# A hand-ordered stage ahead of an RWKV-7 recurrence: scaled vectors moved between key tiles, mixes between gate products, triangular substitution spread over all receptance tiles on one engine

## The chip, the cores and the metric

The kernel runs on one core of a Trainium2 chip. The metric is device time in microseconds (us) of one execution, the median over several runs. Five engines work side by side, each through its own queue in order: PE (TensorE, the matmuls; PEld is its weight load), DVE (VectorE), ACT (ScalarE), POOL (GpSimd) and SP (SyncE, which issues the DMAs).

## What is computed

Two layers on a sequence of 512 tokens of width 1024: a gated short convolution with a squared-ReLU MLP, then an RWKV-7 time mixer with a second MLP. The change lies in the mixer, between its norm and its recurrence. From the normed `h` it computes, per token, six mixes of a token with the one before, and from these the vectors that the recurrence needs:

```python
h_prev = jnp.pad(h, ((0, 0), (1, 0), (0, 0)))[:, :-1]
xr, xw, xk, xv, xa, xg = h[None] + (h_prev - h)[None] * mu[:, None, None, :]
r, k, v = jnp.einsum('nbsd,nde->nbse', jnp.stack([xr, xk, xv]), w_rkv)
w = -jax.nn.softplus(-(w0 + jnp.tanh(xw @ w1) @ w2)) - 0.5
a = jax.nn.sigmoid(a0 + (xa @ a1) @ a2)
g = jax.nn.sigmoid(xg @ g1) @ g2
kk = heads(k * k_k); kk = kk / jnp.maximum(jnp.sqrt(jnp.sum(kk * kk, -1, keepdims=True)), 1e-12)
k = k * (1 + (a - 1) * k_a)
decay = jnp.exp(-jnp.exp(heads(w)))
y = _wkv7_scan(rh, decay, kh, vh, -kk, kk * ah)   # state <- state*w + (state a) b^T + v k^T, y = state r
```

## The kernel before

Activations lie feature-major: 1024 features are 8 blocks of 128 partitions, 512 tokens in the free dimension. A linear layer runs tile by tile: one tile is 128 output features, 8 blocks deep, and each weight and activation is kept as a high and a low part, so that `passes` (L171 to L173) issues three matmuls per block, 24 per tile. For each weight tile SP loads `raw` (two buffers), ACT rounds the high part (L131, cast) and DVE subtracts the low part (L132); `w_ahead` keeps this two tiles in front of PE.

The scan is done in 8 chunks of 64 tokens. For each chunk a 64x64 triangular system has to be inverted; its two 32x32 halves are inverted by substitution (`substitute`: for t from 30 down to 1, one multiply L849 and one add L853 on a block of t rows and 31-t columns), and joined by two small matmul levels (`inverse_level`). The stage ahead of the recurrence has these steps, which the string `PLAN` puts in an order by hand, one letter each; the order on PE is the order of the program, the other engines' queues are ordered by a scheduler:

- `K` key tile, of which five of eight are made with the norm before (`linear(NFIRST, ...)`); `key` copies the tile and squares it (ACT L601); `f` (`flush`) sums the squares per head on PE (L605); `n` (`inv_norms`) takes square roots (ACT L622) and reciprocals (DVE) of all that are there; POOL spreads a norm over its head's columns (L617)
- `T` output of the small decay and rate products, `W` their second product (PE L681) with sigmoids on ACT (L685, L686)
- `L` one block of the gate's small product (L631, L632, L672), `U`, `G` its second weights, `a`, `A` its sigmoid
- `s` (`scaled`) one of eight sets of scaled vectors: PE transposes the norm (L720), DVE multiplies (L723), scans the decay (L712), ACT takes two exponentials (L714, L715) and `m` (L725), DVE L726, L727, L729, L731 and POOL L730 multiply
- `c` (`chunk_matrix`) the triangular matrices of 8 chunks on PE (L753), masked by DVE (L755), written to memory; `b`, `B` load them back, transposed to one matrix per partition
- `X` a receptance mix (`xr_mix`), `R` a receptance tile, ended by a DVE product (L804), `p` a spill of four tiles' vectors to memory, `g` a gate tile (L819, L820, ACT L822)

What is left of the R tiles after `PLAN` runs in a loop that puts substitution steps and the value mixes (`xv`) beside them. In it the substitution is split over DVE and POOL, and the first DVE step after a tile is tied behind the last weight split issued (`behind`, `wst["last"]`). Then `order(0)` prepares the first two heads' blocks (`prestage` L1037 to L1057, `values`/`turned` L1018, L1016 and ACT L1025, `bonus`, `turned_blocks` L968, `inverse_level`, `corrected` L1003), with two value tiles in it, and the recurrence begins (`step`, L1081). During the recurrence `SIDE` and `MSTEP` set how much other work is put between its steps. Here is the loop:

```python
for i in range(done["R"], KB):
    j = r_tile()
    ...
    after = wst["last"]
    while t > 0 and subst + work(t) / 2 < total * (i - 1) / (KB - 2):
        substitute(t, after); after = None
        ...
```

## Time and profile before

| | us |
|---|---|
| median of 3 runs | 1376.19 (1375.8 to 1378.82) |
| the profiled execution | 1376.09 |
| its span in the trace | 1374.3 |
| PE busy, of the span | 1308.5 (95%) |
| DVE / ACT / POOL busy | 843.7 / 543.9 / 197.5 |
| mean granted TensorE clock | 0.973 |

PE is busy nearly all the time, so the kernel's time is PE's work plus what PE waits and what it loses at its lower clock. In the page's 40 slices (34.4 us each) PE stands at 9 or more nearly everywhere; the slices that stand out lie between 653 and 790 us, in the stage that the change rewrites, where it shows 8, 9, 6, 6. A slice tells only a share; the stage is read below by windows, by what PE waited for, and by the instructions themselves.

### The profile page before, as it was taken

What the parts mean: (1) busy time and instruction counts of PE and PEld (TensorE: products, weight loads), DVE (VectorE), ACT (ScalarE), POOL (GpSimd) and SP (SyncE); (2) the same over time, 40 slices, a digit from 0 to 9 for tenths busy, and PEclk for the clock granted to TensorE, in tenths of its full rate; (3) what the DMA queues carried; (4) which work ended last, traced back from release to release, by engine and by line L of the source; (5) the groups of instructions that cost most, each with busy time, mean ns of one, the idle gap of its engine ahead of it and who ended that gap; (6) DMA issues with size and microseconds to landing.
All of it is one profiled execution on the core that took longest, in us unless ns stands there. A gap on an engine that the chain in (4) does not pass through costs nothing. (4 is left out here: it accounts for less than half of the span.)

```text
span 1374.3 us, 20369 instructions
## 1 busy us (share of the span) xinstructions
PE 1308.5 (95%) x8182; PEld 1071.0 (78%) x8182; DVE 843.7 (61%) x1272; ACT 543.9 (40%) x922; POOL 197.5 (14%) x241
## 2 busy tenths in 40 slices
PE   7999999999999999999896699999989999999997
PEld 5788888888888888886675477777778888888886
DVE  7987677747658466736869835566585344343445
ACT  4333344223132243547362356864344132231331
POOL 0000020000000004623438412232300000000000
PEclk9999999999999999999898699999999999999999
DMA  9565524735547355202283513331122322322331
GB/s 369 214 232 197 186 93 157 272 123 212 201 169 260 123 184 183 97 32 73 77 245 78 122 34 124 109 105 51 62 77 77 104 96 92 100 99 92 97 103 62
DMA packets 83582, 184.96 MB, mean 135 GB/s; under 512 B 35392, under 2 KB 37696, under 8 KB 83488
## 3 DMA queue, kind: packets, MB, share of 16 engines
q1 hardware_dynamic: 83488, 183.66, 39.6%
q8 instruction: 64, 1.05, 0.3%
q14 instruction: 30, 0.25, 0.1%
HBM read 168.96 MB, written 13.63 MB: 133 GB/s over the span
## 5 line engine op out<-in xcount | busy, mean ns | idle before, releaser
L173 PE MATMUL ps<-b,w 128*128 128x512 f32 (+1 forms) x1486 | 566.2, 381 | 10.7 <-DVE w L132 9.4
L171 PE MATMUL ps<-b,w 128*128 128x512 f32 (+1 forms) x1486 | 574.3, 387 | 1.4 <-DVE b L304 1.2
L172 PE MATMUL ps<-b,w 128*128 128x512 f32 (+1 forms) x1486 | 566.9, 381 | 4.3 <-POOL b L132 4.3
L131 ACT CAST w<-raw 128x1024 fp32r<-128x1024 f32 x176 | 185.2, 1053 | 488.3 <-PE ps L172 438.5
L173 PEld LDWEIGHTS ps<-b,w 128*128 128x128 f32 x1486 | 282.1, 190 | 64.7 <-DVE w L132 10.1
L172 PEld LDWEIGHTS ps<-b,w 128*128 128x128 f32 x1486 | 282.5, 190 | 57.1 <-POOL b L132 7.5
L171 PEld LDWEIGHTS ps<-b,w 128*128 128x128 f32 x1486 | 282.0, 190 | 57.5 <-issue 3.4
L132 DVE TENSOR_TENSOR w<-raw,w 128x1024 fp32r<-128x1024 f32 x172 | 210.9, 1226 | 147.5 <-ACT w L131 142.2
L304 DVE SCALAR_TENSOR_TENSOR b<-ps,mod,b 128x512 f32<-128x512 f32 (+1 forms) x116 | 80.3, 694 | 174.6 <-PE ps L173 174.2
L205 DVE CUSTOM_DVE_ANT_0 b<-b,b,vec 128x1024 f32<-128x1024 f32 x96 | 122.9, 1281 | 9.7 <-DMA b<-in_ada 8.9
L131 ACT CAST b<-t 128x512 fp32r<-128x512 f32 (+1 forms) x113 | 65.7, 591 | 102.4 <-DVE t L349 80.9
L132 DVE TENSOR_TENSOR b<-t,b 128x512 fp32r<-128x512 f32 x82 | 56.8, 697 | 28.3 <-ACT b L131 28.3
L530 POOL TENSOR_TENSOR b<-b,vec 128x512 f32<-128x512 f32 (+2 forms) x4 | 5.1, 1288 | 322.6 <-DMA b<-in_l 322.6
L132 POOL TENSOR_TENSOR b<-raw,b 128x1024 fp32r<-128x1024 f32 x9 | 22.1, 2464 | 199.6 <-ACT b L131 199.6
L258 ACT ACTIVATE b<-t,mod 128x256 fp32r<-128x256 f32 (+2 forms) x56 | 29.4, 537 | 51.0 <-DVE t L257 50.9
L171 PE MATMUL ps<-b,b 128*128 128x256 f32 (+1 forms) x152 | 46.9, 316 | 1.8 <-ACT b L258 1.7
L349 DVE TENSOR_TENSOR t<-t 128x512 f32<-128x512 f32 x64 | 43.5, 685 | 7.3 <-ACT t L348 7.3
L233 DVE TENSOR_TENSOR t<-t,t 128x256 f32<-128x256 f32 (+1 forms) x47 | 41.5, 884 | 7.9 <-ACT t L232 7.1
L172 PE MATMUL ps<-b,b 128*128 128x256 f32 (+1 forms) x152 | 44.5, 294 | 1.8 <-POOL b L132 1.8
L173 PE MATMUL ps<-b,b 128*128 128x256 f32 (+1 forms) x152 | 44.3, 292 | 0.0
L434 PE MATMUL ps<-b,b 128*128 128x512 f32 x168 | 39.9, 395 | 1.6 <-ACT b L258 1.6
L1025 ACT COPY b<-ps 64x256 f32<-64x256 f32 x96 | 35.3, 367 | 15.5 <-PE ps L1018 11.7
(204 smaller groups left out, 1331.6 us busy)
## 6 DMA issues: line engine op xcount, KB each, us to landing
raw<-in_wmain SPq DMA_DIRECT2D x185, 512.0 KB, 3.3
b<-in_ada SPq DMA_DIRECT2D x96, 512.0 KB, 5.8
sp<-b SPq DMA_DIRECT2D x8, 512.0 KB, 3.4
b<-sp SPq DMA_DIRECT2D x8, 512.0 KB, 4.5
b<-in_cin_a SPq DMA_DIRECT2D x8, 448.0 KB, 9.7
b<-in_x SPq DMA_DIRECT2D x8, 256.0 KB, 5.5
xs<-b SPq DMA_DIRECT2D x8, 256.0 KB, 2.1
sc<-t SPq DMA_DIRECT2D x8, 256.0 KB, 3.1
```

The source lines that it names most:

```text
L131: A.copy(dst_hi, src)
L132: return (eng or V).tensor_tensor(dst_lo, src, dst_hi.bitcast(F32), op=ALU.subtract)
L171: PE.matmul(dst, whi, ahi, start=start, stop=False)
L172: PE.matmul(dst, whi, alo, start=False, stop=False)
L173: return PE.matmul(dst, wlo, ahi, start=False, stop=stop)
L205: return V.tensor_tensor_reduce(junk, w, cb, 1.0, vv(f"ab{l}{v}", m), ALU.mult, ALU.add, mods[l, v][:, m:m + 1])
L233: add[0] = V.tensor_tensor(acc[:, sl], acc[:, sl], t[:, :w], op=ALU.add)
L258: A.activation(hi[:, sl], t[:, :w], AF.Identity, bias=sh[:, k:k + 1])
L304: V.scalar_tensor_tensor(x[m][:, sl], pt[:, sl], gt[:, m:m + 1], x[m][:, sl], op0=ALU.mult, op1=ALU.add)
L349: V.tensor_tensor(r, r, r, op=ALU.mult)
L434: PE.matmul(pts[i], a[:, i * P:(i + 1) * P], h[k][b], start=k == 0 and a is whi and not b, stop=k == KB - 1 and b == 1)
L1025: held(A.copy(dst[:, :, par], src) if (hh ^ par) in TA[n] else V.tensor_copy(dst[:, :, par], src))
```

## The change

`PLAN` gets another order: the key norms are summed and their roots taken right after the first five key tiles, the remaining three key tiles stand among the second products, scaled vectors and chunk matrices, the gate blocks `L` come after them with the receptance mixes between, and no R, spill or gate tile is left in `PLAN`. All eight R tiles run in the loop, each followed by one gate tile, one value mix and a seventh of the substitution (`NSUB` 7, so it is to end beside the seventh); two value tiles follow directly (`NVEARLY`). The substitution runs on DVE alone, both halves in one instruction, with the mask moved to POOL (`affine_select` on the loaded matrices). ACT takes over the copy of the chunk matrix, all first halves of the mixes and the halves `tanh` needs; DVE takes over POOL's `m*ei` and the low parts of the mixes. Sigmoid is written as `0.5*tanh(0.5x)+0.5`, with the factors folded in where they can be. Two 8 KB tiles share one buffer (`x2`). `SIDE[0]` falls from 2.0 to 1.5, and `ORDERS[0]` puts the inverse after the values. The mathematics is the same.

```diff
-NBIG, NTMP, NRAW, NCV = 36, 9, 2, 3
+NBIG, NTMP, NRAW, NCV = 34, 9, 2, 3
-MSTEP, SIDE = (6.75, 6.5, 5.75, 2.75), (2.0, 1.0, 2.6, 2.2)
+MSTEP, SIDE = (6.75, 6.5, 5.75, 2.75), (1.5, 1.0, 2.6, 2.2)
-PLAN = "TXfXKXffXKXffXKXffXffnWWLWWLWWLWWLsLsLcsLcsLcsUcRscRpsGcpaAscRcbpggggBgggg"
+PLAN = "TfffffnWWsKlWsfcWKscfWscKWscfnWscsUWcscLLXcBLLXXLLXXLLXXaGAX"
+NVEARLY, NSUB, USUB = 2, 7, 0.06
-MIXG = {0: 'GAVAAAAG', 7: 'GGGGGGGV'}
-ORDERS = ('a b2 b v i k l I4 I w z c y d', ...
+ORDERS = ('a b2 b v k l w z y i I4 I w c d', ...
-    cb = big((P, D), F32)
-    junk = big((P, D), F32)
+    cj = pool.tile([P, 2, D], F32, tag="x2", name="cj", bufs=1)
+    cb, junk = cj[:, 0], cj[:, 1]
...
-gate_loads()
-gate_scale()          # now step "l" of PLAN
...
-            A.activation(ar[j][:, 1], pw, AF.Sigmoid, bias=vv("w0", j))
-            sg[0] = A.activation(kb[j][:, 1], pa, AF.Sigmoid, bias=vv("a0", j))
+            A.activation(ar[j][:, 1], pw, AF.Tanh, scale=0.5, bias=hw0[:, j:j + 1])
+            A.activation(ar[j][:, 1], ar[j][:, 1], AF.Identity, scale=0.5, bias=half1)
+            A.activation(kb[j][:, 1], pa, AF.Tanh, scale=0.5, bias=ha0[:, j:j + 1])
...
-            behind(A.activation(ei, e, AF.Exp, scale=C0), sg[0])
+            A.activation(ei, e, AF.Exp, scale=C0)
...
-            V.tensor_tensor(bt, bt, ei, op=ALU.mult)
-            V.scalar_tensor_tensor(bt, al, -1.0, bt, op0=ALU.mult, op1=ALU.mult)
+            V.scalar_tensor_tensor(bt, bt, 1.0, ei, op0=ALU.add, op1=ALU.mult)
+            V.scalar_tensor_tensor(bt, al, -0.5, bt, op0=ALU.mult, op1=ALU.mult)
-            G.tensor_tensor(m, m, ei, op=ALU.mult)
+            V.tensor_tensor(m, m, ei, op=ALU.mult)
...
-            V.tensor_tensor(ab, pab, mask[:, 0].unsqueeze(1).broadcast_to([P, NCH, 64]), op=ALU.mult)
+            A.copy(ab, pab)
...
+        def substitute(t):
+            X2, tm = Xs[0], tms[0]
+            w = 31 - t
+            sh = [P, 2, t, w]
+            tv = tm[:, :2 * t * w].rearrange("p (q s c) -> p q s c", q=2, s=t)
+            V.tensor_tensor(tv, X2[:, :, :t, t:t + 1].broadcast_to(sh), X2[:, :, t:t + 1, t + 1:].broadcast_to(sh),
+                            op=ALU.mult)
+            V.tensor_tensor(X2[:, :, :t, t + 1:], X2[:, :, :t, t + 1:], tv, op=ALU.add)
+        def advance(part):
+            if not tms:
+                tms.append(tmp())
+                for q in range(2):
+                    X = Xs[0][:, q]
+                    G.affine_select(out=X, in_=X, pattern=[[-1, 32], [1, 32]], compare_op=ALU.is_gt, fill=0.0, ...)
+                    G.memset(X.rearrange("p s t -> p (s t)")[:, 0:1024:33], 1.0)
+            while steps and subst[0] + work(steps[0]) / 2 / total < part:
+                t = steps.pop(0)
+                substitute(t)
+                subst[0] += work(t) / total
...
-            mix(0, k, FULL, *xr[k], eng=ENGS[MIXG[7][k]], eng_u=ENGS[MIXG[0][k]])
+            mix(0, len(xr) - 1, FULL, *xr[-1])
...
+        def beside_tile(i, mixes):
+            while len(xv) < mixes:
+                xv.append(pair())
+                mix(3, len(xv) - 1, FULL, *xv[-1])
+            if steps:
+                advance(sub0 + (1 - sub0) * (i + 1) / NSUB)
+                if not steps:
+                    nc.sync.dma_start(sc2.rearrange("q p s t -> p q s t"), Xs[0])
+        for i in range(nr):
+            j = r_tile()
+            while done["p"] < min(done["R"], KB // 2):
+                spill()
+            gates()
+            if j < 2:
+                He[j] = big(dt=F32)
+                nc.sync.dma_start(He[j][0:64], ar[j][0:64])
+            beside_tile(i, KB * (i + 1) // nr)
+        inverted()
+        for i in range(NVEARLY):
+            while len(vdone) <= i:
+                next(side)
+            beside_tile(nr + i, KB)
```

How instructions move is seen best in the queues. First PE, among the scaled vectors, before: transposes of the norm (L720) stand between the gate's blocks (L631, L632, L672), the second products are long done, and a chunk matrix (L753) follows two sets later.

```order
L720 MATMUL ps_5006<-ident,t_4999 128x128 x4
L631 MATMUL ps_4931<-b_4177,b_4686 128x512
L632 MATMUL ps_4931<-b_4177,b_4687 128x511
L672 MATMUL ps_4932<-b_4177,b_4689 128x512
L720 MATMUL ps_5029<-ident,t_5011 128x128 x4
L631 MATMUL ps_4931<-b_4177,b_4686 128x512
L632 MATMUL ps_4931<-b_4177,b_4687 128x511
L672 MATMUL ps_4932<-b_4177,b_4689 128x512
L753 MATMUL ps_5047<-b_4919,b_4696 64x64 x16
L720 MATMUL ps_5072<-ident,t_5034 128x128 x4
L631 MATMUL ps_4931<-b_4178,b_4686 128x512
```

After, on PE at the same kind of place (line numbers are those of the changed kernel: L724 is the transpose, L757 the chunk matrix, L684 the second product):

```order
L724 MATMUL ps_5129<-ident,t_5122 128x128 x4
L757 MATMUL ps_5144<-b_4979,b_4702 64x64 x16
L724 MATMUL ps_5169<-ident,t_5134 128x128 x4
L684 MATMUL ps_5190<-b_4709,b_4025 128x512
L684 MATMUL ps_5190<-b_4709,b_4026 128x512
L684 MATMUL ps_5191<-b_4709,b_4064 128x512
L684 MATMUL ps_5191<-b_4709,b_4065 128x512
L757 MATMUL ps_5200<-b_5063,b_4818 64x64 x16
L724 MATMUL ps_5225<-ident,t_5174 128x128 x4
L757 MATMUL ps_5238<-b_5118,b_4926 64x64 x16
L635 MATMUL ps_5258<-b_4179,b_4821 128x512
L636 MATMUL ps_5258<-b_4179,b_4822 128x511
```

The gate's blocks no longer lie between a transpose and the chunk matrix that needs its result; second products and other sets' transposes do, and the gate's blocks follow all transposes.

Next DVE beside the R tiles, before. L849 and L853 are the last steps of a batch of substitution, L132 on `w` is the low part of the weight of a coming R tile, L804 ends an R tile:

```order
L853 TENSOR_TENSOR b_5461<-b_5461,b_5544 128x17x6
L853 TENSOR_TENSOR b_5460<-b_5460,b_5544 128x17x14
L849 TENSOR_TENSOR b_5544<-b_5461 128x112
L849 TENSOR_TENSOR b_5544<-b_5460 128x240
L853 TENSOR_TENSOR b_5461<-b_5461,b_5544 128x16x7
L853 TENSOR_TENSOR b_5460<-b_5460,b_5544 128x16x15
L132 TENSOR_TENSOR w_5716<-raw_5661,w_5715 128x1024
L804 TENSOR_TENSOR b_4928<-b_4928,ps_5690 128x512
```

After, on DVE between two tile ends (L840); L772 and L774 are the substitution's multiply and add, L132 on `w` the weight's low part, L502 and L132 on `b` a value mix:

```order
L840 TENSOR_TENSOR b_5118<-b_5118,ps_5501 128x512
L774 TENSOR_TENSOR xs_5292<-xs_5292,t_5428 128x2x22x9
L132 TENSOR_TENSOR w_5581<-raw_5530,w_5580 128x1024
L772 TENSOR_TENSOR t_5428<-xs_5292 128x420
L502 SCALAR_TENSOR_TENSOR t_5544<-b_4180,vec,t_5544 128x511
L774 TENSOR_TENSOR xs_5292<-xs_5292,t_5428 128x2x21x10
L772 TENSOR_TENSOR t_5428<-xs_5292 128x440
L132 TENSOR_TENSOR b_5543<-t_5544,b_5543 128x512
L774 TENSOR_TENSOR xs_5292<-xs_5292,t_5428 128x2x20x11
L772 TENSOR_TENSOR t_5428<-xs_5292 128x456
L840 TENSOR_TENSOR b_5196<-b_5196,ps_5555 128x512
```

Where 36 substitution rows (of which the last six are shown) stood between one tile end and the next weight's low part, a weight's low part now follows each tile end within two rows, and six substitution rows stand between these two tile ends.

Last ACT, at the first second products, before, where L622 is the root of all eight norms, L685 and L686 the sigmoids:

```order
L622 ACT_TABLE_LOAD
L622 ACTIVATE rn<-ps_4354 128x64
L685 ACT_TABLE_LOAD
L685 ACTIVATE b_4919<-ps_4913,vec 128x512
L686 ACTIVATE b_4696<-ps_4914,vec 128x512
L685 ACTIVATE b_4928<-ps_4922,vec 128x512
L686 ACTIVATE b_4699<-ps_4923,vec 128x512
```

After, where L626 is the root of the first five norms, L688 to L690 the tanh form, L718 to L721 the first scaled vectors:

```order
L626 ACT_TABLE_LOAD
L626 ACTIVATE rn<-ps_4358 128x4x10
L688 ACT_TABLE_LOAD
L688 ACTIVATE b_4751<-ps_4745,half 128x512
L690 ACTIVATE b_4690<-ps_4746,half 128x512
L689 ACTIVATE b_4751<-b_4751,half_1641 128x512
L688 ACTIVATE b_4761<-ps_4755,half 128x512
L690 ACTIVATE b_4693<-ps_4756,half 128x512
L689 ACTIVATE b_4761<-b_4761,half_1641 128x512
L718 ACTIVATE t_4768<-b_4751 128x512
L729 ACTIVATE t_4780<-b_4690,half 128x512
```

The exponentials of the first scaled vectors now follow the first two second products at once, without another table load; there are three activations for a second product where there were two.

## Rows read from the trace of the kernel before

**Rows 1.** Busy time by window: window, its length, PE, PEld, DVE, ACT, POOL, clock, DMA, GB/s
```profile
604.60:629.50 24.90, 23.79 (x137) 20.73 (x137) 17.56 (x16) 20.59 (x34) 11.40 (x8) 1.00 0.26 85
629.50:673.80 44.30, 38.97 (x231) 23.71 (x230) 34.68 (x39) 27.91 (x47) 16.65 (x14) 0.89 0.20 51
673.80:709.80 36.00, 33.53 (x249) 26.67 (x248) 21.72 (x31) 17.23 (x26) 8.49 (x12) 0.94 0.71 180
709.80:741.50 31.70, 22.39 (x99) 18.20 (x97) 27.41 (x57) 11.92 (x18) 22.31 (x39) 0.92 0.45 149
741.50:768.00 26.50, 21.70 (x177) 15.56 (x177) 26.50 (x62) 4.46 (x6) 22.78 (x32) 0.84 0.32 85
768.00:800.10 32.10, 24.05 (x254) 19.27 (x254) 16.90 (x26) 16.22 (x42) 5.58 (x8) 0.68 0.52 116
800.10:993.00 192.90, 186.87 (x2450) 143.75 (x2449) 111.28 (x211) 115.27 (x285) 54.75 (x75) 0.98 0.25 83
```

**Rows 2.** What PE waited for, 604.6 to 800.1: total us, times, longest
```profile
PE ps L173 <- DVE w L132: 9.4, 1, 9.4
PE ps L753 <- DVE b L729: 5.6, 4, 2.3
PE ps L172 <- POOL b L132: 4.3, 6, 2.8
```

**Rows 3.** DVE in order of time: start, us, what it did
```profile
740.07 1.43 DVE L132 TENSOR_TENSOR w<-raw,w 128x1024 fp32r<-128x1024 f32 x1
```

**Rows 4.** All engines in order of time, end of the substitution
```profile
755.85 10.24 POOL L132 TENSOR_TENSOR b<-t,b 128x512 fp32r<-128x512 f32 x8
756.07 2.47 DVE L849 TENSOR_TENSOR b<-b 128x150 f32<-128x150 f32 x2
...
766.12 0.41 DVE L849 TENSOR_TENSOR b<-b 128x108 f32<-128x108 f32 x2
...
766.45 0.42 DVE L853 TENSOR_TENSOR b<-b,b 128x108 f32<-128x108 f32 x2
```

**Rows 5.** DVE in order of time, during the scaled vectors
```profile
641.44 2.38 DVE L712 TENSOR_TENSOR_SCAN b<-cmask,b 128x512 f32<-128x512 f32 x2 [2.04 <-ACT b L685]
...
654.81 1.09 DVE L726 TENSOR_TENSOR b<-b,t 128x512 f32<-128x512 f32 x1
...
668.67 0.68 DVE L726 TENSOR_TENSOR b<-b,t 128x512 f32<-128x512 f32 x1
669.28 0.68 DVE L731 TENSOR_TENSOR b<-b,t 128x512 f32<-128x512 f32 x1
```

**Rows 6.** ACT in order of time, from the root of the norms
```profile
629.60 1.28 ACT L622 ACT_TABLE_LOAD   x1
...
631.13 1.28 ACT L685 ACT_TABLE_LOAD   x1
632.43 0.69 ACT L685 ACTIVATE b<-ps,vec 128x512 f32<-128x512 f32 x1
633.01 0.68 ACT L686 ACTIVATE b<-ps,vec 128x512 f32<-128x512 f32 x1
```

**Rows 7.** PE in order of time, key tiles to scaled vectors
```profile
611.89 1.84 PE L605 MATMUL ps<-blk,b 128*128 128x2 f32 x16
...
619.17 1.84 PE L605 MATMUL ps<-blk,b 128*128 128x2 f32 x16
...
644.08 2.39 PE L681 MATMUL ps<-b,b 128*128 128x512 f32 x8
...
648.88 0.60 PE L720 MATMUL ps<-ident,t 128*128 128x128 f32 x4
...
681.91 1.15 PE L753 MATMUL ps<-b,b 64*64 64x64 f32 x32
```

**Rows 8.** ACT in order of time, after the value tile
```profile
773.82 6.05 ACT L1025 COPY b<-ps 64x256 f32<-64x256 f32 x16 [5.61 <-PE ps L1018]
```

**Rows 9.** POOL, the scaling of small weights: instructions, ns least, median and most
```profile
L530 POOL TENSOR_TENSOR b<-b,omu x4: 794/1041/2083, 518.3 to 579.7; 128x512 f32<-128x512 f32 x2, 128x1024 f32<-128x1024 f32 x1, 128x256 f32<-128x256 f32 x1
```

More of the change, by code (lines that the diff above doesn't have):

```diff
@@ L482, in trunk @@
                     op0=ALU.mult, op1=ALU.add)
-    oka = const.tile([P, KB], F32, name="oka")
-    V.tensor_scalar(oka, vv("ka"), -1.0, 1.0, op0=ALU.mult, op1=ALU.add)
+    half1 = const.tile([P, 1], F32, name="half1")
+    G.memset(half1, 0.5)
+    half = const.tile([P, 4, KB], F32, name="half")
+    hka, oka, hw0, ha0 = (half[:, i] for i in range(4))
+    for dst, n, f, o in ((hka, "ka", 0.5, 0.0), (oka, "ka", -0.5, 1.0), (hw0, "w0", 0.5, 0.0), (ha0, "a0", 0.5, 0.0)):
+        V.tensor_scalar(dst, vv(n), f, o, op0=ALU.mult, op1=ALU.add)
     h = []
@@ L739, in chunk_back @@
             if not Xs:
-                Xs.extend(big((P, 32, 32), F32) for _ in range(2))
+                Xs.append(pool.tile([P, 2, 32, 32], F32, tag="x2", name="xs2", bufs=1))
             jr = slice(16 * j0, 16 * j1)
             for q in range(2):
-                nc.sync.dma_start(Xs[q][jr], sc1[jr, 32 * q:32 * q + 32, 32 * q:32 * q + 32])
+                nc.sync.dma_start(Xs[0][jr, q], sc1[jr, 32 * q:32 * q + 32, 32 * q:32 * q + 32])
         def chunk_matrix():
@@ L754, in chunk_matrix @@
             ab = tmp().rearrange("p (c t) -> p c t", t=64)
-            V.tensor_tensor(ab, pab, mask[:, 0].unsqueeze(1).broadcast_to([P, NCH, 64]), op=ALU.mult)
+            A.copy(ab, pab)
             nc.sync.dma_start(sc1.rearrange("(j g r) s t -> (r s) j g t", j=KB, r=2)[:, j], ab)
-        g2, gahl, xr = [], [], []
+        work = lambda t: 150 + 2 * t * (31 - t)
+        steps, tms = list(range(30, 0, -1)), []
+        total, subst = sum(map(work, steps)), [0.0]
+        def substitute(t):
[11 more added lines that the diff above has]
+                    X = Xs[0][:, q]
+                    G.affine_select(out=X, in_=X, pattern=[[-1, 32], [1, 32]], compare_op=ALU.is_gt, fill=0.0, base=0,
+                                    channel_multiplier=0)
+                    G.memset(X.rearrange("p s t -> p (s t)")[:, 0:1024:33], 1.0)
[3 more added lines that the diff above has]
+                subst[0] += work(t) / total
+        g2, gahl = [], []
         def gate_loads2():
@@ L775, in gate_part, with sigmoid @@
             A.copy(outs[1][32:64, 1:], pt[32:64, :T - 1])
+        def sigmoid(dst, src):
+            A.activation(dst, src, AF.Tanh, scale=0.5)
+            V.tensor_scalar(dst, dst, 0.5, 0.5, op0=ALU.mult, op1=ALU.add)
         def gate_in():
@@ L801, in r_tile @@
             j = RORDER[step_of("R")]
-            assert done["s"] > j and done["X"] == KB
+            assert done["s"] > j and len(xr) == KB
             pr = linear(1, xr)[0]
@@ L901, in even @@
                     held(nc.sync.dma_start(t.rearrange("p n t -> p (n t)"), sp[j - KB // 2, i]))
-        for X in Xs:
-            G.memset(X.rearrange("p s t -> p (s t)")[:, 0:1024:33], 1.0)
-        t = 30
-        work = lambda t: 150 + t * (31 - t) if t > 0 else 0
-        total, subst = sum(map(work, range(31))), 0
-        xv = []
-        for i in range(done["R"], KB):
-            j = r_tile()
-            while done["p"] < min(done["R"], KB // 2):
-                spill()
-            if j < 2:
-                He[j] = big(dt=F32)
-                nc.sync.dma_start(He[j][0:64], ar[j][0:64])
-            after = wst["last"]
-            while t > 0 and subst + work(t) / 2 < total * (i - 1) / (KB - 2):
-                substitute(t, after)
-                after = None
-                subst += work(t)
-                t -= 1
-                if t == 0:
-                    inverted()
-            while i >= 6 and len(xv) < (i - 5) * 4:
-                xv.append(pair())
-                mix(3, len(xv) - 1, FULL, *xv[-1], eng=G)
-        for g in range(4):
-            for par in range(2):
-                nc.sync.dma_start(TT[g][64 * par:64 * par + 32, :, 32:], s1u[0:32, par, g, :, 32:])
-        vt, bo, vdone = {}, {}, set()
+        vt, bo, vdone, xv = {}, {}, set(), []
         def v_tile(j):
@@ L1247, in x_back @@
         def x_back():
-            x[:] = blocks()
+            xy = pool.tile([P, 2, 2, T], F32, tag="x2", name="xy", bufs=1)
+            t = [xy[:, 0], xy[:, 1], big(dt=F32), big(dt=F32)]
+            x[:] = [t[k // 2][:, k % 2] for k in range(KB)]
             for k in range(KB):
```

57 lines of the change are left out of this document (24 added, 33 removed).

## The prediction

> **What bounds the kernel now.** I read the page's slices first, then the busy time by windows over the stage, then the list of what PE waited for, and last the queues of PE, DVE, ACT and POOL in order of time. The stage runs from the end of the first five key tiles (604.6 us) to the first step of the recurrence (800.1 us): 195.5 us. In its six windows PE is busy 23.8 + 39.0 + 33.5 + 22.4 + 21.7 + 24.1 = 164.4 us, so it idles 31.1 us [rows 1]. The longest waits are one of 9.4 us for a weight's low part, 5.6 us in four pieces for scaled vectors, 4.3 us in six pieces for value mixes on POOL [rows 2]; eight more groups share the rest. The 9.4 us end when L132 on DVE has run at 740.07 [rows 3]: that split of the next receptance weight stood behind a batch of substitution. The mixes on POOL and the substitution on DVE then hold each other up: two DVE multiplies of 150 columns take 2.47 us while POOL runs L132, two of 108 columns 0.41 us when POOL is done [rows 4].
>
> Beside idling, PE loses work at half clock: the granted clock is 0.89, 0.94, 0.92, 0.84 and 0.68 in the windows from 629.5 on [rows 1]. If the slow part fell evenly on busy time, the loss would be 0.11 x 39.0 + 0.06 x 33.5 + 0.08 x 22.4 + 0.16 x 21.7 + 0.32 x 24.1 = 19 us; if it fell on idle time wherever it could, 11 us. I take 13, near the lower end, because the low windows are those with the most idle time. So the stage is 164.4 - 13 = 151.4 us of PE work at full clock, and 44 us that something could win. After the stage PE idles only 6.0 us in 192.9 [rows 1], so that a gain made before it is not given back there by a free engine.
>
> **Prices.** A tile of 24 matmuls: from one L605 group to the next, 619.17 - 611.89 = 7.28 us, less some 1.7 of the group itself, is 5.6 us; one matmul 0.233 us, a gate tile of four 0.93. Two second products take 2.39 us, one 1.2; a transpose group 0.60; a chunk matrix 1.15; one gate block (646.47 to 648.88) about 2.5 [rows 7]. On DVE the next instruction starts 0.61 us after one of 512 columns, a scan takes half of 2.38, that is 1.2 [rows 5]. Two instructions of 108 and 76 columns (the halves of one substitution step) take 0.33 from start to start [rows 4]; a line through both, 0.07 + 0.00104 x columns, gives 1.13 for a weight's split of 1,024. On ACT 512 columns take 0.58 from start to start, a table load 1.28 [rows 6].
>
> **Step 1, norms taken early.** The first five groups of norms and their root come before the first second product. Of the work (5 x 0.9 of norms, 2.4 for two second products, 0.6 for a transpose: 7.5 us) nothing hides the chain root, reciprocal, POOL copy, transpose any more, where three key tiles and the gate blocks hid it before. Followed through the queues, ACT has three copies and five squares (8 x 0.58 = 4.6), two casts 1.2, a table load 1.28 and the root; then DVE, POOL and PE have some 0.7 each: 4.6 + 1.2 + 1.5 + 2.1 = 9.4 us. **Wait: 1.9.**
>
> **Step 2, scaled vectors between key tiles.** From there to the first receptance tile PE has 3 key tiles 16.8, six second products 7.2, three groups of norms 2.7, seven transposes 4.2, eight chunk matrices 9.2, eight gate blocks 20, gate assembly 1: 61 us. DVE has eight sets of 0.61 x 6 + 1.2 = 4.9 (one more than before, the product taken from POOL; the mask has gone), that is 39, four weight splits (4.5), eight mixes at 1.25 (10), gate weights and sigmoids 4: 57.5. ACT has per tile three activations and a copy for the second product and chunk matrix, three and a short copy for the set: 7 x 0.58 = 4.1, times 8 is 33; key tiles 3.5, weight casts 4, a second root with its two table loads 2.8, mixes 9.5, gate 6: 59. Three engines with nearly the same load hand work to each other, so PE cannot run through. In the changed order I find PE waiting in four places: at the second root (norms of tiles 5 to 7, two table loads on the path) 2.2; at the chunk matrices of sets 5 and 6, where DVE is behind, 3.3 and 1.3; at the gate assembly, whose copies stand behind the weight casts on ACT, 1.2 to 3.4, of which 2.3. Before, the same vectors held PE for 5.6 us [rows 2]; that is in the 31. POOL's scaling of the gate's weights now falls among the sets: two instructions of 2.08 and two of about 0.8 us [rows 9]. A DVE product beside a POOL instruction took 1.09 instead of 0.68 [rows 5]: 0.4 for each of twelve POOL instructions (these and eight copies of norms) is 5 us of DVE time, of which I put 2 on PE. **Wait: 11.** Bounds 4 (only the root and the assembly) and 27 (rival B). The gate weights' loads go to SP earlier than they are needed by 20 us of PE work. The matrices come back in two loads after the last chunk matrix, and POOL masks them; nearest is its product of 1,024 columns, 2 x 2.08 [rows 9], and fifteen us of gate blocks and the first receptance tile hide both.
>
> The Trainium skill, "SBUF — State Buffer", "SBUF: two separate sides", speaks against moving POOL's work here: a DVE instruction with two SBUF inputs and a POOL instruction that reads SBUF exclude each other for their whole length. The traces show both: 1.24 us for each of the two multiplies of 150 columns beside POOL's 1.28 agree with it [rows 4], 1.09 us beside a POOL instruction of 1.7 does not [rows 5].
>
> The Trainium skill, "ScalarE: Activation LUTs", "What ACT_TABLE_LOAD costs", counts a drain of about 1.38 us with every switch of tables. Here the activation starts 0.02 us after the load has ended [rows 6]. By the page four switches would add 5.5 us to ACT and the estimate would be some 3 us higher; I go by the row.
>
> **Step 3, substitution beside all receptance tiles.** Eight tiles with a gate tile each are 8 x (5.6 + 0.93) = 52 us on PE, 6.5 per tile. The substitution is 60 instructions on twice t(31-t) columns, 19,840 columns in all. By the line above that is 60 x 0.07 + 20.6 = 25 us, 3.5 beside each of seven tiles. With the weight's split 1.13, the tile's product 0.61 and a mix 1.25, DVE has 6.5 per tile, the same as PE. Weights are split two tiles ahead, so DVE may fall behind by more than one tile before PE waits, and the eighth tile has no substitution. POOL is empty there. On SP eight spills and nine weights of 512 KB and eight gate tiles of 256 KB, 11 MB in 52 us, are 210 GB/s; the window from 673.8 moved 180 at a DMA share of 0.71 [rows 1], so they fit, and a late weight has two tiles of slack. **Wait: 0**, bounds 0 and 8 (0.13 more for each of 60 instructions). The 9.4 us go, and the 4.3 for mixes with them.
>
> **Step 4, the end of the stage.** Two value tiles, a third of a tile's first block and the two prestages (11.2 + 0.7 + 4.8 = 16.7) run while the substitution ends about 10 us after the eighth tile; the 6.7 that are left, and the copies below, hide its way through memory and the transpose. Then ACT has 24 copies at 6.05 / 16 = 0.38, 9.1 us [rows 8], ahead of the copies that the inverse needs; before, a value tile stood between those. I count 18 us from the last prestage to the first step against 13 of PE work. **Wait: 5**, bounds 2 and 9.
>
> **The sum.** Waits 1.9 + 11 + 0 + 5 = 18, against 31. Half clock: as it follows idle time here, 13 x 18/31 = 7.5; bounds 2 and 13. The stage becomes 151.4 + 18 + 7.5 = 177, that is 18.6 shorter. `SIDE[0]` moves some 4 us of PE work out of the first recurrence stage, which is full, to later ones that hold 6 us of idle time [rows 1]: between 2 lost and 4 won, I take 1.5 won. The other edits (buffers, table constants, order of the first loads) cost nothing that PE sees: they lie beside matmuls that run without a gap. Sum against the profiled execution: 1376.1 - 18.6 - 1.5 = **1356 us**. That execution is 0.1 us from the median, and 1.8 of its time lies outside the span; I change neither.
>
> **Rivals.**
> A, the stage nearly closes: DVE and ACT run ahead, PE waits only for the roots and the copies of step 4 (8 us) and keeps its clock (2 us). Stage 161.4, 34 shorter, time 1342. For it: the sums of DVE and ACT lie below PE's. Against: each set passes PE, DVE, ACT, POOL and PE again.
> B, DVE is held up by POOL and ACT throughout step 2: 1.09 instead of 0.68 for 40 products is 16 us more, waits 34, clock 10. Stage 195, time about 1374. For it: POOL and DVE hold each other up fully there [rows 4]. Against: POOL has twelve instructions there, not 40. This is what the rule of the Trainium skill's "SBUF — State Buffer" would make of it if POOL were busy throughout.
> C, DVE becomes the bound beside the receptance tiles, with the upper price of step 3: 8 more, time 1364.
> D, slower: the long substitution instructions run at the price of those beside POOL, 1.24 us each, because operands of four dimensions cost as much as a blocked port. Then 60 x 1.24 = 74 instead of 25 us, DVE 13.6 per tile against 6.5, 49 us more, time 1405. It turns slower from 0.75 us per instruction on. Against it: the adds in before, on strided blocks of 150 and fewer columns, cost what the multiplies do [rows 4].
> E, the change does not do what it says: a missing buffer holds a mix or a key tile back, and gains and waits cancel, within 3 us of 1376.
>
> **How the numbers follow.** Forecast 0.50 with its own range 1347 to 1366 (waits 12 to 25, clock 4 to 11); A 0.17, B 0.12, C 0.12, D 0.05, E 0.04. For 8 in 10 the range takes in the forecast, C, most of A and a part of B: 1343 to 1369. About 0.2%, 2.7 us, is what a measurement of this kernel tells from none. Faster: forecast, A, C and most of B, 0.88; within it 0.05; slower D and a rest of B and E, 0.07.
>
> **What would show it.** Right: no PE wait above 3 us for a weight's low part or a POOL mix after 690 us; the first receptance tile at about 687 us and the recurrence begun at about 780; waits of L757 for DVE L733 of some 5 us; ACT's L1023 copies ending just before the inverse. Step 3 is wrong if an L774 of 480 columns takes over 0.7 us, or the substitution ends more than 15 us after the eighth tile; step 2 is wrong if the first receptance tile starts before 675 or after 700. The whole is wrong if the recurrence itself gets longer by more than 2 us.

## The result and the profile after

The changed kernel takes 1364.16 us (median of 6 runs, 1363.43 to 1368.71), against 1376.66 for the kernel before (6 runs): a ratio of 0.9916, 95% interval 0.9900 to 0.9932. Forecast were 1356, range 1343 to 1369. So the sign and the range held, and of the 20.1 us that the sum promised 12.5 came. The profiled execution took 1364.0, its span is 1362.3, 12.0 shorter than before.

The stage, window by window (columns as in [rows 1], to which these rows answer):

```profile
603.20:628.00 24.80, 22.88 (x130) 20.03 (x130) 15.69 (x19) 20.86 (x36) 9.77 (x9) 0.75 0.17 56
628.00:650.00 22.00, 21.45 (x185) 17.61 (x183) 20.59 (x28) 18.25 (x31) 3.19 (x1) 0.97 0.40 125
650.00:664.00 14.00, 8.73 (x113) 6.97 (x114) 11.59 (x18) 11.42 (x21) 1.78 (x3) 0.74 0.75 232
664.00:689.90 25.90, 24.56 (x83) 10.70 (x83) 15.83 (x22) 13.97 (x25) 4.11 (x5) 0.94 0.51 83
689.90:742.60 52.70, 52.70 (x225) 43.30 (x225) 47.52 (x81) 24.02 (x34) 4.17 (x8) 0.97 0.48 155
742.60:759.40 16.80, 16.80 (x180) 13.94 (x179) 14.63 (x28) 6.08 (x10) 1.90 (x1) 1.00 0.59 145
759.40:780.50 21.10, 15.32 (x231) 13.67 (x230) 7.62 (x11) 15.94 (x43) 3.69 (x7) 0.76 0.56 124
```

The stage begins 1.4 us earlier than before and the recurrence starts at 780.5, so it takes 177.3 us instead of 195.5. PE is busy 162.4 of them and idles 14.9; before, it was busy 164.4 and idled 31.1, so nearly all of the gain is idle time. From the first receptance tile (689.9) to the last prestage (759.4) it does not idle at all. What it waited for in the stage, which answers to [rows 2] (line, awaited line: total us, times, longest):

```profile
PE ps L757 <- DVE b L733: 4.4, 3, 2.1
PE ps L985 <- ACT t L980: 3.9, 2, 3.6
PE ps L724 <- POOL t L621: 2.5, 1, 2.5
PE ps L821 <- ACT t L806: 1.3, 1, 1.3
PE ps L1014 <- DVE b L1052: 1.1, 2, 0.8
PE ps L609 <- ACT b L605: 0.8, 1, 0.8
PE ps L1001 <- ACT b L987: 0.8, 1, 0.8
```

No wait for a weight's low part or a value mix is left. L757 waits for the scaled vectors, L724 for the second root, L985 for the inverse behind ACT's copies.

One execution does not fix the length of this stage. The runs e1 and e6 below issue, up to the recurrence, the same instructions as the changed kernel in the same order on PE, DVE, ACT and POOL, and their stages take 173.1 and 173.0 us, at a granted clock of 0.92 instead of 0.89 and with 14.6 and 14.7 us of idle time. The stage of e1 as one window:

```profile
604.80:777.90 173.10, 158.46 (x1139) 123.39 (x1139) 133.51 (x203) 110.61 (x196) 28.75 (x34) 0.92 0.49 131
```

But from the first recurrence step to the end of the span the changed kernel needs 7.6 us more. That stretch of the kernel before, by window:

```profile
800.10:1374.30 574.20, 553.81 (x4213) 453.00 (x4211) 290.04 (x458) 235.69 (x454) 59.57 (x77) 0.99 0.27 89
```

its longest PE waits up to the last MLP (its lines stand two further down the file than the changed kernel's):

```profile
PE ps L1100 <- ACT uv L1083: 3.3, 2, 2.3
PE ps L251 <- DVE t L248: 2.0, 1, 2.0
```

The same window of the changed kernel:

```profile
780.50:1362.20 581.70, 556.43 (x4212) 454.51 (x4211) 288.99 (x457) 231.94 (x448) 64.62 (x77) 0.98 0.26 87
```

and its longest waits there:

```profile
PE ps L1079 <- DVE b L1102: 3.1, 3, 2.0
PE ps L251 <- DVE t L248: 2.9, 1, 2.9
PE ps L1152 <- ACT t L1145: 1.7, 1, 1.7
```

PE idle goes from 13.7 to 18.7 us, summed over the gaps between its instructions (some 6.7 us behind its last one are in neither number); the other 2.6 are longer busy time for the same work. So the account of the span is: 1.4 won ahead of the stage, 18.2 in it, 7.6 lost behind it, 12.0 in all. The 1.4 are not told from nothing: in the runs below, whose instructions ahead of the stage are the changed kernel's, it starts between 602.3 and 606.6. My sum had 18.6 in the stage and 1.5 won behind it. The term behind the stage is far off, and the runs go there first.

### The profile page after: what moved, and what is told of

Same layout as the page of the kernel before. It is cut to its first block, busy times and chain, and to the rows that moved or that the text cites. A ratio compares the mean times of both kernels' runs of the same rounds, so it can differ in the third digit from the quotient of the medians.

```text
span 1362.3 us, 20211 instructions
## 1 busy us (share of the span) xinstructions
PE 1309.3 (96%) x8182; PEld 1074.0 (79%) x8182; DVE 829.4 (61%) x1249; ACT 552.2 (41%) x941; POOL 137.7 (10%) x159
## 4 chain that ended last, share of the span: by engine, by line
PE 87%; DVE 6%; ACT 4%; issue 1%; DMA 1%; POOL 0%; SPq 0%; DVEq 0%; ACTq 0%
PE ps L171 25%; PE ps L172 24%; PE ps L173 24%; DVE t L233 2%; PE ps L1001 1%; PE ps L1046 1%; PE ps L434 1%; PE ps L635 1%; PE ps L636 1%; ACT b L1023 1%; PE ps L1079 1%; ACT w L131 1%; PE ps L1115 1%; PE ps L1098 1%; PE ps L609 1%
## 5 line engine op out<-in xcount | busy, mean ns | idle before, releaser
L173 PEld LDWEIGHTS ps<-b,w 128*128 128x128 f32 x1486 | 281.2, 189 | 55.9 <-POOL w L132 1.7
L132 DVE TENSOR_TENSOR w<-raw,w 128x1024 fp32r<-128x1024 f32 x172 | 211.9, 1232 | 146.9 <-ACT w L131 141.3
L205 DVE CUSTOM_DVE_ANT_0 cj<-b,cj,vec 128x1024 f32<-128x1024 f32 x96 | 122.9, 1280 | 11.4 <-DMA b<-in_ada 10.6
L304 DVE SCALAR_TENSOR_TENSOR b<-ps,mod,b 128x512 f32<-128x512 f32 (+1 forms) x84 | 56.3, 672 | 117.8 <-PE ps L173 117.5
L132 DVE TENSOR_TENSOR b<-t,b 128x512 fp32r<-128x512 f32 x97 | 66.3, 692 | 27.2 <-ACT b L131 27.2
L304 DVE SCALAR_TENSOR_TENSOR xy<-ps,mod,xy 128x512 f32<-128x512 f32 x32 | 24.0, 750 | 62.2 <-PE ps L173 62.2
L132 POOL TENSOR_TENSOR b<-raw,b 128x1024 fp32r<-128x1024 f32 x9 | 22.0, 2459 | 200.5 <-ACT b L131 200.5
L348 ACT ACTIVATE t<-ps 128x512 f32<-128x512 f32 x64 | 37.1, 587 | 7.3 <-PE ps L173 7.3
```

Of the source, the lines that this page charges most:

```text
L132: return (eng or V).tensor_tensor(dst_lo, src, dst_hi.bitcast(F32), op=ALU.subtract)
L173: return PE.matmul(dst, wlo, ahi, start=False, stop=stop)
L205: return V.tensor_tensor_reduce(junk, w, cb, 1.0, vv(f"ab{l}{v}", m), ALU.mult, ALU.add, mods[l, v][:, m:m + 1])
L304: V.scalar_tensor_tensor(x[m][:, sl], pt[:, sl], gt[:, m:m + 1], x[m][:, sl], op0=ALU.mult, op1=ALU.add)
L348: A.activation(r, pt, AF.Relu)
```

## Experiments

Each label's edit is against the changed kernel, unless said otherwise. Runs sent together share a chip and the runs of the kernel before, so the ratios to it are compared across the three groups. Differences in the text are of medians; by the ratios e1, e5 and e9 come out 8.1, 9.1 and 16.2 us below the changed kernel instead of 6.8, 8.1 and 12.8, and e4, e7 and e11 3.9, 8.1 and 22.4 above it instead of 4.4, 9.3 and 24.7. No run takes back the early norms, the moved key tiles or the form of the sigmoid alone, so what each of these is worth is not shown.

| run | edit | us, median (lowest to highest) | ratio to before, 95% |
|---|---|---|---|
| changed | | 1364.16 (1363.43 to 1368.71) | 0.9916 (0.9900 to 0.9932) |
| e1 | SIDE[0] 2.0 | 1357.34 (1354.43 to 1358.91) | 0.9857 (0.9843 to 0.9870) |
| e2 | before, SIDE[0] 1.5 | 1387.45 (1381.48 to 1388.69) | 1.0068 (1.0053 to 1.0084) |
| e3 | SIDE[0] 2.5 | 1365.59 (1360.30 to 1369.59) | 0.9916 (0.9896 to 0.9935) |
| e4 | half the turned copies on DVE | 1368.55 (1366.69 to 1373.28) | 0.9944 (0.9930 to 0.9958) |
| e5 | gate blocks into the waits | 1356.09 (1353.19 to 1358.54) | 0.9850 (0.9831 to 0.9870) |
| e6 | NSUB 2 | 1365.23 (1363.39 to 1366.72) | 0.9917 (0.9904 to 0.9931) |
| e7 | value mixes on POOL | 1373.48 (1370.07 to 1376.54) | 0.9975 (0.9961 to 0.9989) |
| e8 | values turned first | 1363.92 (1362.69 to 1365.36) | 0.9908 (0.9894 to 0.9922) |
| e9 | e1 and e5 | 1351.39 (1343.79 to 1353.38) | 0.9798 (0.9775 to 0.9822) |
| e10 | e1, e5 and e8 | 1347.20 (1343.98 to 1350.90) | 0.9781 (0.9760 to 0.9803) |
| e11 | batches ahead of the splits | 1388.85 (1385.60 to 1392.45) | 1.0079 (1.0061 to 1.0097) |

### The time lost behind the stage: SIDE[0] in both kernels

```diff
-MSTEP, SIDE = (6.75, 6.5, 5.75, 2.75), (1.5, 1.0, 2.6, 2.2)
+MSTEP, SIDE = (6.75, 6.5, 5.75, 2.75), (2.0, 1.0, 2.6, 2.2)
```

The kernel after with the old value, the kernel before with the new one, and the kernel after with 2.5:

> The changed kernel with SIDE[0] back at 2.0; from the first recurrence step to the end TensorE's instructions then stand as in the kernel before. In the trace of the changed kernel the recurrence and the tail take 581.8 us, 7.6 more than before. Theory (the smaller SIDE[0] moved work out of the first recurrence group into places that wait): the 7.6 us go, 1356 to 1357 us, first step of the recurrence still at 780.5. Rival (the 7.6 us come from the new stage itself: its buffers, the order of its last copies, the state in which it leaves the engines): 1364 us, recurrence and tail still about 582.

> The kernel before with SIDE[0] at 1.5 and nothing else changed; from the first recurrence step on TensorE's instructions then stand as in the changed kernel. Theory (the smaller SIDE[0] costs the time): 7 to 8 us slower than before, 1384 us. Rival (the stage ahead costs it): 1376 us, no change. My prediction's own term for this edit was 1.5 us faster, 1375.

> The changed kernel with SIDE[0] at 2.5, more of the value and output projections between the steps of the first recurrence group than in either kernel. Theory (each unit taken out of the first group comes back with waits): no slower than SIDE[0] at 2.0, 1353 to 1358 us. Rival (2.0 is where the first group is just full, more only lengthens it): 1359 to 1364 us.

The new stage with the old value gains 6.8 us more, the old stage with the new value loses 10.2. From the first recurrence step to the end, by window, in e1:

```profile
777.90:1352.60 574.70, 553.45 (x4212) 453.51 (x4211) 289.53 (x457) 232.33 (x447) 60.56 (x77) 0.99 0.27 88
```

with these as its longest waits:

```profile
PE ps L1098 <- ACT uv L1081: 3.2, 2, 2.1
PE ps L251 <- DVE t L248: 2.0, 1, 2.0
```

The window in e2:

```profile
800.30:1386.80 586.50, 561.29 (x4213) 458.68 (x4211) 289.03 (x458) 234.64 (x454) 63.87 (x77) 0.97 0.27 87
```

and its waits (line numbers as in the kernel before):

```profile
PE ps L1081 <- DVE b L1104: 3.5, 4, 2.0
PE ps L251 <- DVE t L248: 2.9, 1, 2.9
...
PE ps L1154 <- ACT t L1147: 1.7, 1, 1.7
```

The waits go with SIDE[0] and not with the stage: e2 has those of the changed kernel within half a microsecond, and e1 those of the kernel before within 0.1, with one more of 1.4 (L1152 for ACT). Every run with 1.5 has a stretch of 581.6 to 586.6 us with 18.5 to 18.8 of PE idle, every one with 2.0 a stretch of 574.2 to 577.4 with 13.7 to 15.0. So the theory holds, and the rival (the stage leaves a burden) falls. The idle time does not make up all of it: in e2 the stretch is 12.3 us longer than before, of which 4.9 are idle and 7.5 longer busy time for the same work, and that busy time also differs between runs with the same SIDE[0] (553.5 us in e1, 556.0 in e9). With 2.5 the stretch is 584.8 long and 18.0 idle: e3's theory missed, and of the three values 2.0 is the best. So it is not simply the amount of work in the first group that costs; my reading, which no run takes apart, is that the number decides which waits of the later groups still have projection work beside them.

### The end of the stage: ACT's row of copies

```diff
-held(A.copy(dst[:, :, par], src) if (hh ^ par) in TA[n] else ...
+held(A.copy(dst[:, :, par], src) if (g or not par) and (hh ^ par) in TA[n] else ...
```

> The changed kernel with half of the 16 turned copies of the first group of heads that go to ACT (L1023) put on DVE, which is busy 7.6 of the last 21.1 us of the stage. Theory (ACT's 24 copies in a row, 9.1 us, hold back the two copies that the inverse waits for): the wait of 3.6 us at L985 falls below 1, and the one of 6.9 us at half clock behind it shrinks; 3 to 6 us faster than the changed kernel, 1358 to 1361. Rival (the masked products of DVE at L1052 and the way through memory end as late): below 1 us, 1363 to 1364.

(It takes 12 of the 24 copies off ACT; the expectation's count of 16 is wrong, its 9.1 us right.) It is 4.4 us slower. PE's longest wait at the end of the stage, in e4:

```profile
PE ps L977 <- DVE b L966: 6.0, 1, 6.0
```

and DVE in order of time (start, length, what it did), in e4:

```profile
766.50 3.74 DVE L1023 COPY b<-ps 64x256 f32<-64x256 f32 x9 [0.43 <-ACT b L1023]
770.27 0.69 DVE L961 TENSOR_TENSOR b<-b,ps 128x512 f32<-128x512 f32 x1
770.99 0.77 DVE L1023 COPY b<-ps 64x256 f32<-64x256 f32 x2
771.79 0.69 DVE L961 TENSOR_TENSOR b<-b,ps 128x512 f32<-128x512 f32 x1
772.39 1.24 DVE L966 STREAM_TRANSPOSE b<-b 128x1024 f32<-128x1024 f32 x1
```

In the changed kernel DVE makes that transpose right behind its masked products:

```profile
763.26 1.23 DVE L966 STREAM_TRANSPOSE b<-b 128x1024 f32<-128x1024 f32 x1
```

The wait at L985 did shrink, from 3.9 to 1.0 in all, as the theory said. But the copies were queued ahead of the transpose that the inverse's first product needs, and a wait of 6.0 took its place. A free engine is not a free place in its queue.

e8 shortens ACT's row without DVE:

```diff
-ORDERS = ('a b2 b v k l w z y i I4 I w c d', ...
+ORDERS = ('a v w b2 b k l z y i I4 I c d', ...
```

> The changed kernel with ORDERS[0] as 'a v w b2 b k l z y i I4 I c d': the turning of the two value tiles and their eight copies on ACT stand between the two prestages instead of around the turned columns, so that 16 copies instead of 24 stand ahead of the inverse's on ACT, and nothing is put on DVE. Theory (it is ACT's row of copies that holds the inverse): the row behind the last prestage is 6.1 us instead of 9.1, the wait at L985 falls from 3.6 to 0.5 to 2 us, the recurrence starts 2 to 3 us earlier, 1361 to 1362. Rival (DVE's masked products at L1052 and its transpose, which stand where they stood, are the bound): start within 0.5 us, 1363.5 to 1364.5.

The median is 0.2 us lower, which the intervals do not tell from nothing; in the profile the recurrence starts 1.25 earlier, of which 0.5 is behind the first receptance tile; but e1 and e6, with the changed kernel's order, need 0.7 less than e8 for that part. The wait at L985 falls only from 3.6 to 2.8. ACT in e8:

```profile
757.65 3.05 ACT L1023 COPY b<-ps 64x256 f32<-64x256 f32 x8 [2.63 <-PE ps L1016]
760.72 1.84 ACT L1075 COPY uv<-b 64x128 f32<-64x128 f32 x6
762.57 6.05 ACT L1023 COPY b<-ps 64x256 f32<-64x256 f32 x16
768.64 1.18 ACT L980 COPY t<-ps 32x512 f32<-32x512 f32 x2
```

and in the changed kernel:

```profile
760.59 9.11 ACT L1023 COPY b<-ps 64x256 f32<-64x256 f32 x24 [4.82 <-PE ps L1016]
769.72 1.18 ACT L980 COPY t<-ps 32x512 f32<-32x512 f32 x2
```

Both rows run without a gap into L980, so ACT is the bound there, as the theory said. Its 3 us did not come because six copies for the first step (L1075, 1.84 us) came ahead of the sixteen.

### The scaled vectors: is PE out of work or are DVE and ACT the bound?

```diff
-...KWscfnWscsUWcscLLXcBLLXXLLXXLLXXaGAX"
+...KWscfnLWscLsUWLcscLXcBLXXLXXLXXLaGAX"
```

> The changed kernel with its PLAN's gate blocks L moved: one each behind the second n, the last second product's neighbours and the last chunk matrices, instead of all eight in the run of mixes after them. Nothing else moves. In the changed kernel TensorE idles 5.3 us between 650 and 664 us, where it waits for the second root and for DVE's scaled vectors. Theory (TensorE has nothing else to do there; DVE is not the bound of the whole stretch): the waits behind L724 and L757 shrink from 5.8 to below 2 us, 3 to 5 us faster than the changed kernel, 1359 to 1361. Rival (DVE and ACT are the bound up to the first receptance tile, and the blocks taken out of the run of mixes leave a hole there): the first receptance tile starts no earlier, 1363 to 1365.

It is 8.1 us faster, more than the theory gave. The window from 650 to 664, in e5:

```profile
650.00:664.00 14.00, 14.00 (x107) 8.35 (x106) 12.06 (x20) 12.12 (x22) 1.79 (x3) 1.00 0.71 217
```

and what is left of the waits for scaled vectors in the stage:

```profile
PE ps L757 <- DVE b L733: 2.8, 2, 1.6
```

The second root's wait (L724, 2.5 us) is gone, that of L757 falls from 4.4 to 2.8, and the clock of the window from 650 is 1.00 instead of 0.74. The first receptance tile starts at 683.6 instead of 689.9, the recurrence at 772.9 instead of 780.5, though in this execution the stage began 3.3 us later (606.5): it takes 166.4 us instead of 177.3. Its stage as one window:

```profile
606.50:772.90 166.40, 154.95 (x1140) 120.07 (x1139) 134.62 (x203) 110.33 (x195) 29.07 (x34) 0.95 0.51 137
```

Against e1 and e6 above it is 6.7 us shorter, of which 3.2 are idle time, and the rest is busy time at a higher clock (0.95 for 0.92). So DVE and ACT (12.1 of 14 us each) were no bound; PE had been given nothing else to do.

### The receptance tiles: what removed the 9.4 us?

Two things changed there: the substitution is dealt out over all tiles, and POOL is left out. e6 and e11 take back the first, e7 part of the second.

```diff
-NVEARLY, NSUB, USUB = 2, 7, 0.06
+NVEARLY, NSUB, USUB = 2, 2, 0.06
```

> The changed kernel with NSUB at 2: the same 60 substitution instructions, but all of them beside the first two of the eight receptance tiles instead of seven, some 12.5 us of DVE time more behind each, where the tile itself takes 6.4. Theory (it is the even spread that lets DVE split every receptance weight in time): TensorE waits again for a weight's low part, 5 to 10 us in the first four tiles, 1369 to 1374 us. Rival (the weights are split far enough ahead; the spread does nothing): no wait, 1363 to 1365, perhaps less as the inverse is ready earlier.

This run decides nothing. DVE's queue is set by the scheduler, not by the order in which the program writes it, and the steps ran as evenly as with 7. It shows that NSUB alone does nothing, and serves as a second sample of the changed kernel. In e11 each weight's split is held behind the steps written ahead of it as well:

```diff
             wst["last"] = split(hi, lo, wst["raw"].pop(i), G if spare else eng)
+            if wst.get("hold") is not None:
+                behind(wst["last"], wst["hold"])
...
-            V.tensor_tensor(X2[:, :, :t, t + 1:], ..., tv, op=ALU.add)
+            wst["hold"] = V.tensor_tensor(X2[:, :, :t, t + 1:], ..., tv, op=ALU.add)
```

> The changed kernel with NSUB at 2 and each weight's split on DVE held behind the substitution steps that the program wrote ahead of it, so that DVE really runs two batches of some 15 us. (With NSUB at 2 alone the scheduler dealt the steps out as evenly as before: they ran from 698.3 to 752.2 us, against 699.3 to 753.3 in the changed kernel.) Theory (the 9.4 us wait of the kernel before came from a split that stood behind a batch, and the even spread is what removes it): TensorE waits for a weight's low part at two or three of the receptance tiles, 8 to 18 us together, 1370 to 1380 us, though the inverse is ready earlier. Rival (the splits have slack enough): under 3 us of waits, 1362 to 1367 us.

It is 24.7 us slower than the changed kernel and slower than the kernel before. PE's longest wait from the first receptance tile on, in e11, whose lines stand two further down:

```profile
PE ps L175 <- DVE w L132: 19.3, 2, 10.6
```

and DVE ahead of its first piece, in order of time:

```profile
715.22 0.66 DVE L774 TENSOR_TENSOR t<-xs 128x480 f32<-128x480 f32 x1
715.91 0.66 DVE L776 TENSOR_TENSOR xs<-xs,t 128x480 f32<-128x480 f32 x1
716.49 1.22 DVE L132 TENSOR_TENSOR w<-raw,w 128x1024 fp32r<-128x1024 f32 x1
```

This is the wait of [rows 2] again, twice, for the reason of [rows 3]: a split of 1.2 us behind a batch. With the same work on the same engine, its order alone costs 19.3 us of waits, more than the 8 to 18 that the theory gave.

e7 gives the low half of each value mix's split back to POOL:

```diff
-                mix(3, len(xv) - 1, FULL, *xv[-1])
+                mix(3, len(xv) - 1, FULL, *xv[-1], eng=G)
```

> The changed kernel with the second half of the split of the eight value mixes (L132) back on POOL, beside the substitution on DVE, as it stood in the kernel before. It takes 8 x 0.68 us from DVE. Theory (POOL and DVE hold each other up there): the substitution instructions that meet a POOL split take up to twice as long, DVE's busy time beside the receptance tiles rises in spite of the work taken off it, TensorE still waits less than 2 us there; 1364 to 1367. Rival (they do not disturb each other once the batches are spread): DVE 5 us less busy, substitution done earlier, 1363 to 1364.

It is 9.3 us slower, beyond what either side expected. POOL and DVE in order of time beside one split, in e7:

```profile
739.36 1.56 POOL L132 TENSOR_TENSOR b<-t,b 128x512 fp32r<-128x512 f32 x1 [5.34 <-ACT b L131]
...
739.80 1.55 DVE L772 TENSOR_TENSOR t<-xs 128x396 f32<-128x396 f32 x1
...
741.39 0.57 DVE L774 TENSOR_TENSOR xs<-xs,t 128x396 f32<-128x396 f32 x1
```

and what PE waited for that is not in the changed kernel's list:

```profile
PE ps L171 <- ACT b L131: 4.9, 1, 4.9
...
PE ps L172 <- POOL b L132: 1.3, 2, 0.7
```

DVE's multiply begins 0.44 us into POOL's split and ends 0.43 after POOL's end at 740.92; the add of the same 396 columns that follows takes 0.57. Seven of the 60 substitution instructions meet a split in this way and take 1.37 to 1.64 us, each ending 0.19 to 0.51 after POOL's. So the substitution's busy time is 36.9 instead of 30.0 us: DVE lost 6.9 where it was relieved of 5.5, and it made the last value mix (L502) at 752.10 instead of 744.96, a tile later. The theory named the mechanism and missed how little slack DVE had to pay for it (55.9 busy of 61.1 us in the changed kernel). Not all of the delay is that mechanism: the scheduler also put 56 of the 60 substitution instructions ahead of this last mix, where the changed kernel has 49. What each of the two cost is not shown.

### Together

> The changed kernel with the two edits that gained alone: the gate blocks L behind the second n and between the last chunk matrices, and SIDE[0] at 2.0. Theory (they act in different stretches and add up): first recurrence step at about 773 us as with the gate blocks alone, recurrence and tail 574 to 575 us as with SIDE[0] at 2.0 alone, together 1348 to 1350 us. Rival (the earlier stage leaves the engines in another state, and the recurrence gives some of it back): 1352 to 1356 us.

> The kernel with the gate blocks moved and SIDE[0] at 2.0, and the value tiles turned between the two prestages as well. Theory (ACT's row of copies begins 2 to 3 us earlier but takes in six copies for the first step, 1.8 us, that stood behind it): 0.5 to 1 us faster than without the last edit, 1347.5 to 1349. Rival (no gain, DVE's and POOL's products end as late): no difference above 0.3 us.

e9 starts the recurrence at 771.2 and needs 577.4 us from there, with the same PE idle as e1 (14.7); its five runs spread from 1343.8 to 1353.4, and the median lies between what theory and rival gave. Alone the two edits gained 6.8 and 8.1, together 12.8: they add up within that spread. e10's intervals overlap with e9's, so the third edit's gain stays open. Both beat the kernel before by about 2% and the changed kernel by about 1%, with intervals apart from the changed kernel's.

## Why the prediction was right, and where it was wrong

**What bounds the kernel: held for the idling.** The loss ahead of the recurrence was PE's idling and its half clock. The gain was made in the idling, which fell by 16.2 us; the half clock cost about as much after as before in these two executions, and some 4 us less in e1 (see below).

**Step 1: the forecast wait did not come, partly by luck.** The 1.9 were to stand ahead of the first transpose, where PE does not wait at all; the 0.8 (L609 for L605) are another wait, for the squares. I had put 4.5 and 2.4 us of norms and second products against a chain of 9.4. PE ran most of them at half clock and took 11.1 us (9.1 in e1), and POOL had the first norm spread at 613.4, 1.7 us before that transpose began. The norms:

```profile
604.04 7.65 PE L609 MATMUL ps<-blk,b 128*128 128x2 f32 x40 [0.81 <-ACT b L605]
```

Before, 16 of these took 1.84 us [rows 7].

**Step 2: right places, smaller waits.** Forecast 2.2 at the second root, 3.3 and 1.3 at the matrices of sets 5 and 6, 2.3 at the assembly, 2 for POOL; measured 2.55, 2.13, 1.14, 1.34 and a further 1.10 at the first set, 8.3 against 11. Of the forty products of DVE two were held up by POOL, in that first set (1.04 and 1.09 us instead of 0.68), so the 2 us put down for POOL are at most part of the 1.10. Three of the eight scans took 1.56, 1.57 and 2.85 us beside POOL instead of 1.22. My reading that 1.09 us stood beside a POOL instruction of 1.7 [rows 5] was wrong. What ran there in the kernel before was this:

```profile
654.29 1.07 POOL L617 TENSOR_SCALAR t<-rn 128x512 f32<-128x512 f32 x1
```

It ended at 655.36, and the product, begun at 654.81, 0.54 us later.

**Step 3: held, its price was low.** The wait is 0, and e11 shows that the even spread does it. The 60 instructions were busy 30.0 us, 28.3 from start to start, where my line through two widths gave 25; 480 columns took 0.66 us, and 0.69 to the start of the next where that needed the result, not 0.57. They still ended 10.7 us after the eighth tile, as forecast, since DVE found room beside the two value tiles. The margin was thin: e7, with 1.4 us more on DVE and the last mix further back in its queue, has 6.2 us of waits, inside the bounds of 0 to 8 that I had put on this step.

**Step 4: held.** 5 forecast, 5.8 measured, 3.9 of them for the reason given (L985 behind ACT's copies): with half of the copies off ACT, in e4, the 3.9 fall to 1.0.

**Half clock and work: both mis-sized, and the stage's 177 is luck.** The granted clock is 0.50, that is 1.2 GHz, in five stretches of the stage before (630.3 to 633.7, 667.9 to 678.1, 736.1 to 746.4, 756.6 to 760.0, 770.3 to 790.7) and in six of the stage after (605.6 to 615.8, 626.1 to 629.5, 653.4 to 656.8, 660.2 to 667.0, 690.9 to 694.3, 769.4 to 779.7). Their sums, before and after:

```profile
sum 47.70, PE 34.56 PEld 27.25 DVE 37.34 ACT 17.02 POOL 21.49; mean PE 6.91 PEld 5.45 DVE 7.47 ACT 3.40 POOL 4.30
sum 37.50, PE 34.23 PEld 28.14 DVE 16.39 ACT 27.17 POOL 4.48; mean PE 5.71 PEld 4.69 DVE 2.73 ACT 4.53 POOL 0.75
```

Matmuls of 512 columns start 0.43 us apart there and 0.23 apart elsewhere, so some 47% of PE's busy time in these stretches is lost: by this estimate 16 us before and 16 after, where I had put 13 and 7.5. The work at full clock is then 146 to 148 us and not 151.4. After, 146 of work, 15 of waits and 16 of half clock make the 177: work and waits came out 5 and 3 us below my terms, the clock 8 to 9 above. I scaled the loss with idle time, which halved while the loss did not. Nor is it fixed by the instructions: in e1 the stretches are 27.3 us, 25.0 of them busy, a loss of 12 beside the same idle time, hence its shorter stage.

In the changed kernel's execution the low clock of 0.75, 0.74 and 0.76 stands in the windows where PE does 40 matmuls of 2 columns in a row, where it waits for the second root, and where it waits for the inverse. In the last, 64 matmuls of L1001 take 6.9 us, 0.108 each, against 0.063 for the 32 of L1046, of the same shape, ahead of the wait.

**SIDE[0]: the step that failed.** I let the 4 us of work taken out of the first recurrence group fill the 6 us of idle time in the later ones, and bounded it between 2 lost and 4 won. It cost 6.8 (e1) to 10.2 (e2). Those 6 us were waits at fixed points between the steps; moving projection work changes what stands beside each of them, and here others came up (at L1079, L251 and several smaller ones) and that at L1098 went, five us more in all. The bound should have come from the idle time that the group of after could gain, not from what that of before had to give. I had named the recurrence's growth by more than 2 us as what would make the whole wrong, but gave it no rival of its own. It grew by 7.6, so by that sign the forecast as a whole is wrong, though its range took in the measured time. Without this edit the changed kernel is at 1357.3, where the sum without its 1.5 gives 1357.5. Why both 1.5 and 2.5 bring up waits that 2.0 does not have was not taken apart further.

**Rivals.** A (the stage nearly closes, 161.4 us) did not come, though e10's stage, from 603.5 to 767.7, is 164.2 long: it was to be had, by filling the waits and not by the change's own order. C's time, 1364, is the one measured, and that is chance: C puts 8 us of waits beside the receptance tiles, where PE does not wait. B, D and E fell: no set was held up throughout, the longest substitution instruction took 0.66 us and not 1.24, and gains and losses did not cancel to within 3 us of 1376.

## What to carry to other kernels

Deal work out in pieces shorter than the slack of what stands behind it in the queue, and check in the trace that the scheduler did so; before moving work to an idle engine, look at what will stand behind it there. A wait on a chain that cannot be shortened is removed by giving TensorE independent work at that very point, and in e5 this paid more than the idle time removed (6.7 us for 3.2 against e1 and e6), as the clock was higher too. A number that shifts work between interleaved stages is a change of its own: time it apart from the rest.
